# Moving the low part of half of each Q from VectorE to GpSimd in a two-layer attention kernel

## The chip, the cores and the metric

One core of one Trainium2 chip runs the program. The metric is the device time of one execution in microseconds. The kernel before took 1781.78 us, the median of three runs (1780.85, 1781.80 and 1781.78 us).

## The reference, cut to what matters

Two layers work on 1024 latent tokens and 256 context tokens of width 1024. Layer 0 is a latent attention with 16 heads. Layer 1, where the change is, is a differential attention with 8 heads:

```python
SEQ, CTX_LEN, B_HEADS, B_HEAD = 1024, 256, 8, 64
# per head two query and two key maps of 64 rows each, and values of 128 rows
q = apply_rope(q, cos, sin)          # x1*cos - x2*sin , x2*cos + x1*sin
p1 = softmax(q1 @ k1.T * HD**-0.5)   # 1024 x 1280
p2 = softmax(q2 @ k2.T * HD**-0.5)
o  = rms_norm((p1 - lam * p2) @ v)   # per head, then gate and output projection
```

The result is wanted in more exact arithmetic than one half-precision product gives. So the kernel writes each float32 operand as a sum of two 16-bit numbers, a high part H = f16(x) and a low part L = f16(x - H), and multiplies the parts that matter.

## The kernel before, in words

**How layer 1 is tiled.** Each head works through eight tiles of 128 query rows against all 1280 keys. For one tile `scores1` makes two score maps on TensorE (lines L1342 and L1343, each a product with the high parts and one with the low parts of Q), VectorE takes row maxima (L1355 for the context columns, four times L1359 for the rest, and L1361 joins them), ScalarE takes the exponentials into two tiles p of 1280 columns (L1365) with their sums, and VectorE joins the two maps into one: L1368, L1369 and L1370 make the factor, and L1371 computes p0 + factor*p1 over 1280 columns. In this text "the join" is L1371. `turn1` then transposes the joined tile on TensorE (L1378, matmuls of 128x128 in float32 from p) and splits the transposed columns into 16-bit parts: ph on ScalarE (L181) and pl on VectorE (L182). `values1` multiplies ph and pl with the values (L1386 to L1388), ScalarE scales and squares the result (L1391, L1392), GpSimd makes the norm (L159, L160, L1390) and scales the rows (L1399), and the SyncE queue writes them out (L1400). A head takes about 96 us.

**The next head's operands.** While one head's tiles run, generators make K, Q and V of the next head, and their matmuls (L185 to L187) fill TensorE between the tiles. `prod_q1` makes Q in two halves of 512 columns, b = 0 and b = 1. Each half is a bank of PSUM with 128 rows (both maps), on which `rope1` works: VectorE shuffles rows into rsw (L1242), multiplies by the cosine into rr (L1243), GpSimd multiplies rsw by the sine (L1244) and adds it (L1245). The function `fin`, which runs at a later slot of the weave, then splits rr, scaled by a column es1[h], with `split16`: ScalarE writes the high part kH (L181), VectorE writes the low part kL = rr*es - kH in one instruction (L182), and eight transfers on the SyncE queue (`dmv`, L86) copy the 64-row pieces into the tiles QS (high part, twice) and Q1 (low part, twice; the profile prints it as Q). K goes the same way at 1280 columns (`prod_k1`, KS).

**What holds the order.** The program's order on TensorE around this place is written by hand. The order on VectorE, ScalarE, GpSimd and the SyncE queue is worked out by a scheduler from the instructions and their dependencies. Each engine and the queue run in their order, so an instruction that waits holds all that stands behind it. The tiles rr, rsw, kH and kL have one buffer each: the second half's L1243 writes the same rr that the first half's split still reads, and the second half's kH and kL wait until the transfers of the first half have read them. TensorE works in eight banks of PSUM, ps_b, in turn.

**Two other users of the same engines.** The weights of the next head come on the SyncE queue (ws<-in_dw, L989), ScalarE squares them for a norm (wsq<-ws, L993) and both are split into wx and wy (L181, L182). A row of gates is collected on VectorE from further weights (L1412 loads them, L1414 is the multiplication and addition over 1024 columns).

Of the kernel before, what the change touches and what calls it, by code (L numbers as in the profile page):

```python
# [13 lines left out]
AF = mybir.ActivationFunctionType  # L14
ALU = mybir.AluOpType
# [38 lines left out]
def hybrid_kernel(  # L54
# [7 lines left out]
    pe, act, dve, pool, sp = nc.tensor, nc.scalar, nc.vector, nc.gpsimd, nc.sync  # L62
# [22 lines left out]
    def dmv(dst, src):  # L85
        sp.dma_start(dst, src)  # L86
# [92 lines left out]
    def split16(hi, lo, src, scale):  # L179

        act.activation(hi, src, AF.Copy, scale=scale)  # L181
        dve.scalar_tensor_tensor(lo, src, scale, hi, op0=ALU.mult, op1=ALU.subtract)  # L182
# [793 lines left out]
    def w1(tag):  # L976
        sh, d, b = TAG1[tag]
        return rot(place[tag], sh, d, tag, b)

    wt, un, us1, es1 = {}, {}, {}, {}  # L980
# [40 lines left out]
    def proj1(n, c0, cw):  # L1021
        w = wt[0]
        ps = bank("b")
        for k in range(KT):
            mm3(ps[:, :n], w[k][0][:, cw], w[k][1][:, cw], h1H[:, k, c0:c0 + n], h1L[:, k, c0:c0 + n],
                k == 0, k == KT - 1)
            yield ps
# [212 lines left out]
    def rope1(ps, n, cos, sin, r):  # L1240
        sw = w1("rsw")
        dve.stream_shuffle(sw[:, :n], ps, SWAP16)  # L1242
        dve.tensor_tensor(r[:, :n], ps, cos, op=ALU.mult)  # L1243
        pool.tensor_tensor(sw[:, :n], sw[:, :n], sin, op=ALU.mult)  # L1244
        pool.tensor_tensor(r[:, :n], r[:, :n], sw[:, :n], op=ALU.add)  # L1245
# [27 lines left out]
    def prod_q1(h, b, ps=None):  # L1273
        c0, n = CHUNKS[b]
        if ps is None:
            for ps in proj1(n, c0, slice(0, P)):
                yield 3 * n
        rr = w1("rr")
        c = slice(c0, c0 + n)
        rope1(ps, n, cosB[:, c], sinB[:, c], rr)  # L1280
        if b == 0:
            qt1[h] = [w1(f"Q1{m}") for m in range(2)], [w1(f"QS{m}") for m in range(2)]
        q1, qs = qt1[h]

        def fin():
            H, L = w1("kH")[:, :n], w1("kL")[:, :n]
            split16(H, L, rr, es1[h])
            for m in range(2):
                r = slice(m * HD, m * HD + HD)
                dmv(qs[m][:HD, c], H[r, :])  # L1290
                dmv(qs[m][HD:, c], H[r, :])
                dmv(q1[m][:HD, c], L[r, :])
                dmv(q1[m][HD:, c], L[r, :])

        later.append(fin)
        yield 0
# [414 lines left out]
```

## Time and profile before

| | |
|---|---|
| median of three runs | 1781.78 us |
| the profiled execution | 1781.43 us |
| its span in the profile | 1779.5 us |
| mean granted TensorE clock | 0.992 |
| busy: PE, DVE, ACT, POOL | 1664.8, 1230.8, 1119.5, 800.3 us |
| layer 1's tiles of heads 0 to 7 | about 945 to 1720 us in the span |

The profiled execution is 1.9 us longer than its span; what lies outside is the same for all sums below. PE is TensorE, PEld its weight loads, DVE VectorE, ACT ScalarE, POOL GpSimd, SPq the SyncE queue of transfers. A row of the timeline gives the start and the length in us, the engine, the line, the operation, the tiles with their sizes, and in brackets how long the engine had idled before it and for whom. A row of the waits gives the waiting instruction, whom it waited for, the sum in us, the number of waits and the longest. A row of the windows gives the stretch, its length, then busy us (and instructions) of PE, PEld, DVE, ACT and POOL, the granted clock, the DMA share and GB/s.

### The profile page before, as it was taken

The page shows a single profiled execution, that of the slowest core. Times are in us where ns is not written, and L with a number is a line of the kernel's source. Part 1 is how long each engine was busy: PE and PEld are TensorE (multiplying, and loading weights), DVE is VectorE, ACT ScalarE, POOL GpSimd, SP SyncE. Part 2 cuts the span into 40 slices and gives each one's busy share as a digit, 9 for nine tenths or more (in the row PEclk, how much of TensorE's full clock was granted, in tenths as well). Part 3 has the DMA queues.
Part 4 walks back from the last instruction along what each step waited for, and adds up shares of the span by engine and source line. Part 5 has one row for each costly group of instructions (what it writes and reads, how often), then busy time and mean ns, then how long its engine had stood idle before and what let it go on. Part 6 is the DMA issues. An engine that isn't in the chain of part 4 may idle for free. (4 is left out here: it accounts for less than half of the span.)

```text
span 1779.5 us, 36756 instructions
## 1 busy us (share of the span) xinstructions
PE 1664.8 (94%) x14564; PEld 1233.5 (69%) x14564; DVE 1230.8 (69%) x2045; ACT 1119.5 (63%) x2235; POOL 800.3 (45%) x724
## 2 busy tenths in 40 slices
PE   7999999899999998999999999999998999888998
PEld 7999966566666665577866766667675757566876
DVE  7658575665665657557747787787777777868664
ACT  2551177777777787845536676767676766758542
POOL 1532147667776676845541222222313131455454
PEclk9999999999999999999999999999999999999999
DMA  8258520111111113164432212131312122232331
GB/s 301 86 151 261 161 68 22 40 46 27 36 45 34 46 42 85 47 217 166 148 108 76 55 50 74 55 79 55 81 55 60 38 61 61 68 119 67 108 110 71
DMA packets 111225, 154.84 MB, mean 87 GB/s; under 512 B 13415, under 2 KB 84679, under 8 KB 111054
## 3 DMA queue, kind: packets, MB, share of 16 engines
q1 hardware_dynamic: 102654, 144.90, 27.1%
q10 hardware_dynamic: 8400, 7.61, 1.3%
q8 instruction: 114, 1.87, 0.5%
q14 instruction: 57, 0.47, 0.1%
HBM read 98.65 MB, written 27.07 MB: 71 GB/s over the span
## 5 line engine op out<-in xcount | busy, mean ns | idle before, releaser
L779 POOL TENSOR_TENSOR pl<-p,ph 128x1024 f16<-128x1024 f32 (+1 forms) x176 | 364.7, 2078 | 146.4 <-ACT ph L778 120.6
L1365 ACT ACTIVATE p<-ps_b,mx 128x512 f32<-128x512 f32 (+1 forms) x384 | 230.7, 618 | 84.0 <-DVE mx L1361 82.9
L777 ACT ACTIVATE p<-ps_a,esc 128x1024 f32<-128x1024 f32 (+1 forms) x176 | 189.2, 1075 | 93.2 <-PE ps_a L835 87.2
L759 DVE TENSOR_REDUCE mx<-ps_a 128x1 f32<-128x1024 f32 x128 | 155.3, 1222 | 126.9 <-PE ps_a L757 126.8
L778 ACT CAST ph<-p 128x1024 f16<-128x1024 f32 (+1 forms) x176 | 177.1, 1006 | 5.5
L1359 DVE TENSOR_REDUCE mx<-ps_b 128x1 f32<-128x512 f32 x256 | 166.0, 681 | 0.3 <-PE ps_b L1343 0.3
L848 PE MATMUL ps_d<-Vh,pl 128*128 128x65 f16 x1344 | 146.0, 194 | 3.3 <-POOL pl L779 3.3
L845 PE MATMUL ps_d<-Vh,ph 128*128 128x65 f16 x1344 | 148.1, 195 | 0.0
L847 PE MATMUL ps_d<-Vl,ph 128*128 128x64 f16 x1344 | 146.9, 193 | 0.0
L845 PEld LDWEIGHTS <-ph 128*128 128x128 f16 x1344 | 123.2, 97 | 18.0 <-issue 4.6
L1342 PE MATMUL ps_b<-KS,QS 128*128 128x512 f16 (+1 forms) x384 | 127.7, 349 | 7.5 <-DVE pl L182 4.1
L1390 POOL TENSOR_TENSOR sm<-sm,us 128x1 f32<-128x1 f32 x64 | 19.3, 302 | 252.7 <-DVE sm L1369 248.3
L847 PEld LDWEIGHTS <-ph 128*128 128x128 f16 x1344 | 123.9, 98 | 12.1
L1378 PE MATMUL ps_b<-idr,p 128*128 128x128 f32 x640 | 104.1, 278 | 29.9 <-ACT p L1365 15.7
L1343 PE MATMUL ps_b<-KS,Q 128*128 128x512 f16 (+1 forms) x384 | 130.5, 349 | 0.0
L833 PE MATMUL ps_a<-qH,KH 100*128 100x512 f16 x320 | 121.5, 380 | 9.0 <-ACT p L777 4.7
L182 DVE SCALAR_TENSOR_TENSOR pl<-ps_b,lcf,ph 128x512 f16<-128x512 f32 (+1 forms) x192 | 117.2, 654 | 13.7 <-ACT ph L181 13.6
L848 PEld LDWEIGHTS <-pl 128*128 128x128 f16 x1344 | 123.1, 97 | 4.6 <-POOL pl L779 4.6
L181 ACT ACTIVATE ph<-ps_b,lcf 128x512 f16<-128x512 f32 (+1 forms) x192 | 115.4, 649 | 17.3 <-PE ps_b L1378 17.3
L834 PE MATMUL ps_a<-qH,KL 96*128 96x512 f16 x320 | 121.3, 379 | 0.0
L835 PE MATMUL ps_a<-qL,KH 96*128 96x512 f16 x320 | 120.7, 377 | 0.0
L1378 PEld LDWEIGHTS ps_b<-idr,p 128*128 128x128 f32 x640 | 77.6, 143 | 57.1 <-ACT p L1365 24.5
(435 smaller groups left out, 5282.2 us busy)
## 6 DMA issues: line engine op xcount, KB each, us to landing
ws<-in_dw SPq DMA_DIRECT2D x28, 512.0 KB, 4.0
adw<-in_ada_w SPq DMA_DIRECT2D x24, 512.0 KB, 4.6
adaw<-in_ada_w SPq DMA_DIRECT2D x16, 512.0 KB, 7.5
g<-sg_d SPq DMA_DIRECT2D x16, 512.0 KB, 9.0
sg_d<-gg ACTq DMA_DIRECT2D x40, 128.0 KB, 3.5
o_d<-op SPq DMA_DIRECT2D x7, 640.0 KB, 3.9
xt<-in_xT SPq DMA_DIRECT2D x16, 256.0 KB, 4.6
wgs<-in_w_in SPq DMA_DIRECT2D x32, 128.0 KB, 2.3
```

Source lines behind the costliest of these rows:

```text
L759: dve.tensor_reduce(mx[:, t, 0:1], ps, axis=AX.X, op=ALU.max)
L777: act.activation(p32[:, :n], st, AF.Exp, scale=esc0)
L778: act.copy(ph[:, :n], p32[:, :n])
L779: pool.tensor_tensor(pl[:, :n], p32[:, :n], ph[:, :n], op=ALU.subtract)
L845: pe.matmul(pv[:, t, :], ph[:, ts], Vh[:, k, h, :], start=(k == kcs[0] and t == 0), stop=False, skip_group_check=True)
L847: pe.matmul(pv[:, t, :V0], ph[:, ts], Vl[:, k, h, :], start=False, stop=False, skip_group_check=True)
L848: pe.matmul(pv[:, t, :], pl[:, ts], Vh[:, k, h, :], start=False, stop=(k == NT - 1), skip_group_check=True)
L1342: pe.matmul(out, qs[m][:, ts], ks[m][:, c0:c0 + n], start=True, stop=False)
L1343: pe.matmul(out, q1[m][:, ts], ks[m][:, c0:c0 + n], start=False, stop=True)
L1359: dve.tensor_reduce(mx[:, 2 + 2 * m + i:3 + 2 * m + i], b, axis=AX.X, op=ALU.max, negate=True)
L1365: act.activation(p[m][:, c0:c0 + n], b, AF.Exp, bias=nb, accum_out=sm[:, 2 + 3 * m + i:3 + 3 * m + i])
L1378: pe.transpose(st[:, j * P:(j + 1) * P], pc[:, (k0 + j) * P:(k0 + j + 1) * P], idn)
```

## The change

In `fin` of `prod_q1`, the first half (b = 0) no longer calls `split16`. ScalarE makes the high part as before. GpSimd then scales rr in place and subtracts the high part from it. The second half stays as it was. The lines behind L1287 move down by five: the join L1371 becomes L1376, the maxima L1355, L1359 and L1361 become L1360, L1364 and L1366, the row scaling L1399 becomes L1404, its transfer L1400 becomes L1405, and the gates' L1414 becomes L1419. The code runs for eight heads, for head 0 ahead of the tiles and for heads 1 to 7 within the tiles of the head before.

```diff
         def fin():
             H, L = w1("kH")[:, :n], w1("kL")[:, :n]
-            split16(H, L, rr, es1[h])
+            if b:
+                split16(H, L, rr, es1[h])
+            else:
+                act.activation(H, rr, AF.Copy, scale=es1[h])
+                pool.tensor_scalar(rr, rr, es1[h], None, op0=ALU.mult)
+                pool.tensor_tensor(L, rr, H, op=ALU.subtract)
             for m in range(2):
```

The scheduler's order changes with it. On GpSimd, where Q of head 2 is made, these rows stand before (rr is the rotated half of Q; ss and o belong to an output tile; the last two rows are the second half's):

```order
L1245 TENSOR_TENSOR rr_14569<-rr_14569,rsw_14570 128x512
L159 TENSOR_SCALAR ss_14683<-ss_14683 128x1
L160 TENSOR_TENSOR ss_14683<-ss_14683,neghalf 128x1
L1399 TENSOR_SCALAR o_2204_14681<-o_2204_14681,ss_14683 128x128
L1244 TENSOR_TENSOR rsw_14728<-rsw_14728,sinB_12501 128x512
L1245 TENSOR_TENSOR rr_14727<-rr_14727,rsw_14728 128x512
```

and these now, at the same place:

```order
L1245 TENSOR_TENSOR rr_14571<-rr_14571,rsw_14572 128x512
L1291 TENSOR_SCALAR rr_14571<-rr_14571,es_13781 128x512
L1292 TENSOR_TENSOR kL_14601<-rr_14571,kH_14600 128x512
L159 TENSOR_SCALAR ss_14686<-ss_14686 128x1
L160 TENSOR_TENSOR ss_14686<-ss_14686,neghalf 128x1
L1404 TENSOR_SCALAR o_2204_14684<-o_2204_14684,ss_14686 128x128
L1244 TENSOR_TENSOR rsw_14731<-rsw_14731,sinB_12501 128x512
L1245 TENSOR_TENSOR rr_14730<-rr_14730,rsw_14731 128x512
```

The two new instructions stand right behind the addition that ends the rotation, and the output tile's norm and the second half's rotation stand behind them.

On VectorE at the same place, from the join of one tile to the shuffle of the second half, before:

```order
L1371 SCALAR_TENSOR_TENSOR p_2162_14437<-p_2163_14438,sm_14436,p_2162_14437 128x1280
L182 SCALAR_TENSOR_TENSOR kL_14599<-rr_14569,es_13779,kH_14598 128x512
L1355 TENSOR_REDUCE mx_14610<-ps_b_14614 128x2
L1359 TENSOR_REDUCE mx_14610<-ps_b_14620 128x1
L1359 TENSOR_REDUCE mx_14610<-ps_b_14638 128x1
L1359 TENSOR_REDUCE mx_14610<-ps_b_14624 128x1
L1359 TENSOR_REDUCE mx_14610<-ps_b_14642 128x1
L1361 TENSOR_SCALAR mx_14610<-mx_14610 128x1 x2
L182 SCALAR_TENSOR_TENSOR pl_14698<-ps_b_14699,lcf,ph_14697 128x512
L1414 SCALAR_TENSOR_TENSOR gate_12517<-ws_15465,sc,gate_12517 128x1024
L1242 STREAM_SHUFFLE rsw_14728<-ps_b_14579 128x512
```

and now:

```order
L1376 SCALAR_TENSOR_TENSOR p_2162_14439<-p_2163_14440,sm_14438,p_2162_14439 128x1280
L1360 TENSOR_REDUCE mx_14613<-ps_b_14617 128x2
L1364 TENSOR_REDUCE mx_14613<-ps_b_14623 128x1
L1364 TENSOR_REDUCE mx_14613<-ps_b_14641 128x1
L1364 TENSOR_REDUCE mx_14613<-ps_b_14627 128x1
L1364 TENSOR_REDUCE mx_14613<-ps_b_14645 128x1
L1366 TENSOR_SCALAR mx_14613<-mx_14613 128x1 x2
L1419 SCALAR_TENSOR_TENSOR gate_12517<-ws_15468,sc,gate_12517 128x1024
L182 SCALAR_TENSOR_TENSOR pl_14701<-ps_b_14702,lcf,ph_14700 128x512
L1242 STREAM_SHUFFLE rsw_14731<-ps_b_14581 128x512
```

kL has left VectorE from between the join and the maxima of the next tile, and the gates' multiplication has come ahead of pl.

On VectorE at the second half of Q of head 1, from its kL on, before:

```order
L182 SCALAR_TENSOR_TENSOR kL_13446<-rr_13417,es_12789,kH_13445 128x512
L1370 SCALAR_TENSOR_TENSOR sm_13301<-sm_13301,nlam 128x1
L1355 TENSOR_REDUCE mx_13457<-ps_b_13461 128x2
L1371 SCALAR_TENSOR_TENSOR p_1988_13302<-p_1989_13303,sm_13301,p_1988_13302 128x1280
L1359 TENSOR_REDUCE mx_13457<-ps_b_13467 128x1
```

and now:

```order
L182 SCALAR_TENSOR_TENSOR kL_13448<-rr_13419,es_12790,kH_13447 128x512
L1374 RECIPROCAL sm_13303<-sm_13303 128x2
L1360 TENSOR_REDUCE mx_13459<-ps_b_13463 128x2
L1375 SCALAR_TENSOR_TENSOR sm_13303<-sm_13303,nlam 128x1
L1364 TENSOR_REDUCE mx_13459<-ps_b_13469 128x1
L1376 SCALAR_TENSOR_TENSOR p_1988_13304<-p_1989_13305,sm_13303,p_1988_13304 128x1280
```

The join has moved behind the first L1364 (the former L1359). The second half of head 6 shows the same. In the second halves of heads 2 to 5 the join has come ahead of that L1364 instead. In head 7's first half, where kL stood between L1370 and the join, one L1364 stands there now. In head 6 the low part of K (L182, 128x1280 from kr) has moved from ahead of the join's factor to behind the first half's cosine product L1243. The order on TensorE is the same as before. On the SyncE queue the eight transfers of each half stay ahead of the output tile's L1405 and, in heads 1 to 4, of a weight load L989; one of the transfers of kH has come ahead of the first two of kL.

## The prediction

> **What bounds the kernel now.** The first view is the page's list of busy times, the second the waits, grouped by who waited for whom.
>
> ```profile
> PE 1664.8 (94%) x14564; PEld 1233.5 (69%) x14564; DVE 1230.8 (69%) x2045; ACT 1119.5 (63%) x2235; POOL 800.3 (45%) x724
> ...
> PE ps_b L1378 <- ACT p L1365: 15.7, 20, 2.0
> ...
> PE ps_b L1378 <- DVE p L1371: 8.3, 8, 4.7
> ...
> DVE kL L182 <- ACT kH L181: 21.5, 13, 3.6
> ```
>
> TensorE is busy for 94% of the span. Whatever VectorE or GpSimd gain counts only where TensorE waits for them. The transposes L1378 wait 15.7 us for exponentials and 8.3 us for joins, and VectorE stands 21.5 us at kL until ScalarE has written kH. So the change can win only where VectorE's stand at kL is passed on to L1378. The third view is the timeline at that place, here head 2, first half:
>
> ```profile
> 1073.95 1.54 DVE L1371 SCALAR_TENSOR_TENSOR p<-p,sm,p 128x1280 f32<-128x1280 f32 x1
> ...
> 1075.94 1.26 POOL L1245 TENSOR_TENSOR rr<-rr,rsw 128x512 f32<-128x512 f32 x1
> ...
> 1077.24 0.72 ACT L181 ACTIVATE kH<-rr,es 128x512 f16<-128x512 f32 x1 [3.68 <-POOL rr L1245]
> ...
> 1078.00 0.75 DVE L182 SCALAR_TENSOR_TENSOR kL<-rr,es,kH 128x512 f16<-128x512 f32 x1 [2.51 <-ACT kH L181]
> ...
> 1078.67 0.68 DVE L1355 TENSOR_REDUCE mx<-ps_b 128x2 f32<-128x512 f32 x1
> ...
> 1079.18 1.19 SPq L86 DMA_DIRECT2D Q<-kL  x2
> 1079.27 2.47 DVE L1359 TENSOR_REDUCE mx<-ps_b 128x1 f32<-128x512 f32 x4
> ...
> 1081.66 0.44 DVE L1361 TENSOR_SCALAR mx<-mx 128x1 f32<-128x1 f32 x2
> ...
> 1081.96 0.69 ACT L1365 ACTIVATE p<-ps_b,mx 128x512 f32<-128x512 f32 x1 [2.73 <-DVE mx L1361]
> ...
> 1082.68 1.27 DVE L1414 SCALAR_TENSOR_TENSOR gate<-ws,sc,gate 128x1024 f32<-128x1024 f32 x1
> 1082.79 0.44 PE L1378 MATMUL ps_b<-idr,p 128*128 128x128 f32 x2 [1.96 <-ACT p L1365]
> ```
>
> The chain reads: GpSimd's addition ends at 1077.20, kH at 1077.96, kL at 1078.75. VectorE had been free since 1075.49. The maxima behind kL end late, the exponentials start late, and TensorE waits 1.96 us. Heads 3, 4 and 5 have the same pattern.
>
> **The change, part by part.** VectorE loses eight kL of 0.75 us, which are worth only what stands behind them. ScalarE's part is the same. GpSimd gains eight scalings and eight subtractions, and the nearest rows to their prices are these:
>
> ```profile
> L1399 POOL TENSOR_SCALAR o<-o,ss x56: 612/612/1400, 978.7 to 1643.0; 128x128 f32<-128x128 f32 x56
> ```
>
> ```profile
> L999 POOL TENSOR_SCALAR uw<-uw x16: 192/192/193, 829.2 to 1546.2; 128x1 f32<-128x1 f32 x16
> ```
>
> ```profile
> L779 POOL TENSOR_TENSOR pl<-p,ph 128x512 f16<-128x512 f32 x16 | 19.6, 1223 | 0.0
> ```
>
> The subtraction has a row of its own form: 1.22 us. No row shows the scaling at 512 columns. Between 1 column (0.192 us) and 128 columns (0.612 us) a column costs 3.3 ns; 0.192 + 511 x 3.3 ns gives 1.88 us. The ends are 0.61 us, if columns past 128 cost nothing, and 2.45 us, four times the 128-column row. I take 1.88 us, since both rows of the form carry it. The Trainium skill, "GPSIMD Engine Reference", section 4.1 on engine selection, says that two-input elementwise work is about twice as slow on GpSimd as on VectorE, while one-input work goes at roughly line rate. By that the scaling would cost about as much as on VectorE, and the sum would be that of the first rival below. The two rows speak against it: 3.3 ns for each further column is more than VectorE's whole kL needs (0.75 us over 512 columns, 1.5 ns).
>
> GpSimd and VectorE hold each other up where VectorE reads two tiles from SBUF:
>
> ```profile
> 1362.78 1.55 DVE L1371 SCALAR_TENSOR_TENSOR p<-p,sm,p 128x1280 f32<-128x1280 f32 x1
> ...
> 1363.41 1.40 POOL L1399 TENSOR_SCALAR o<-o,ss 128x128 f32<-128x128 f32 x1
> ```
>
> The 0.61-us scaling of an output row stretches to 1.40 us and ends 0.48 us after the join that ran beside it. So I let such pairs run one after the other.
>
> **Heads 2, 3 and 4.** VectorE no longer stands at kL. It takes the maxima from 1075.5 on as TensorE delivers them, is through by about 1078.9, and the exponentials start at about 1079.2 instead of 1081.96. The 1.96-us wait goes. What is late next is the low part itself. kH ends at 1077.96, the scaling runs to 1079.9. The gates' L1414, now ahead of pl, gets in between the two GpSimd instructions (1.27 us, to 1081.2), and the subtraction ends at 1082.5, 3.7 us later than kL did. On the SyncE queue five transfers from there on hang behind it (0.6 us each, from 1.19 for two), then the row's L1400 and the weight load L989:
>
> ```profile
> 1083.98 0.39 SPq L989 DMA_DIRECT2D ws<-in_dw  x1
> ...
> 1087.97 1.04 ACT L993 ACTIVATE wsq<-ws 128x1024 f32<-128x1024 f32 x1
> ...
> 1092.45 0.69 ACT L1365 ACTIVATE p<-ps_b,mx 128x512 f32<-128x512 f32 x1 [1.92 <-DVE mx L1361]
> ```
>
> L989 is issued at about 1086.3 instead of 1083.98. It took 4.0 us until L993 could read it, so L993 starts at 1090.3. On ScalarE the copy and the output's L1391 and L1392 follow (with L993 some 2.2 us), and the exponentials come at 1092.5 against 1092.45. The gain is given back by the next tile: **0 us** each. A microsecond on the subtraction's end is a microsecond here, up to the wait itself: from -2.0 (scaling 0.61, and the subtraction then ahead of the gates' step) to +0.6 (2.45) per head.
>
> **Head 5** has neither a gates' step nor a weight load there.
>
> ```profile
> 1371.62 0.66 PE L1378 MATMUL ps_b<-idr,p 128*128 128x128 f32 x2 [1.97 <-ACT p L1365]
> ```
>
> ```profile
> 1370.00:1380.00 10.00, 8.38 (x68) 6.36 (x69) 7.47 (x16) 5.63 (x16) 3.09 (x3) 0.83 0.28 68
> ```
>
> Its wait of 1.97 us goes, and the window that it begins ran at a clock of 0.83, 1.7 us lost of 10. The later second half takes back an estimated 0.8 us: **-2.9 us**.
>
> **Head 1** has no such wait to win, only what comes later:
>
> ```profile
> 982.74 0.75 DVE L182 SCALAR_TENSOR_TENSOR kL<-rr,es,kH 128x512 f16<-128x512 f32 x1 [1.16 <-ACT kH L181]
> ...
> 985.15 1.28 DVE L1414 SCALAR_TENSOR_TENSOR gate<-ws,sc,gate 128x1024 f32<-128x1024 f32 x1
> ...
> 990.93 0.74 DVE L182 SCALAR_TENSOR_TENSOR kL<-rr,es,kH 128x512 f16<-128x512 f32 x1
> ...
> 992.33 1.54 DVE L1371 SCALAR_TENSOR_TENSOR p<-p,sm,p 128x1280 f32<-128x1280 f32 x1
> ...
> 994.24 0.60 PE L1378 MATMUL ps_b<-idr,p 128*128 128x128 f32 x4
> ```
>
> ```profile
> Q<-kL SPq DMA_DIRECT2D x64, 64.0 KB, 2.0
> KS<-kL SPq DMA_DIRECT2D x16, 160.0 KB, 5.2
> ```
>
> The scaling starts where kL did and ends at 984.65; the gates' L1414, 0.75 us earlier than now, comes next (to 985.9), and the subtraction ends at about 987.1. The second half's kL may write its one buffer only when the first half's transfers have read it: five at 0.6 us and 2.0 us to land, about 992.0 instead of 990.93. Then come L1355 and, newly, one L1359 of 0.6 us ahead of the join, which ends at 995.65 instead of 993.87. TensorE's transposes start there instead of at 994.24: **+1.4 us**.
>
> **Head 6** loses more order than time on GpSimd:
>
> ```profile
> 1454.91 1.54 DVE L182 SCALAR_TENSOR_TENSOR kL<-kr,kc,kH 128x1280 f16<-128x1280 f32 x1
> ...
> 1467.95 0.67 DVE L1243 TENSOR_TENSOR rr<-ps_b,cosB 128x512 f32<-128x512 f32 x1
> ...
> 1474.46 1.54 DVE L1371 SCALAR_TENSOR_TENSOR p<-p,sm,p 128x1280 f32<-128x1280 f32 x1
> ```
>
> K's low part, moved behind L1243 of the first half, ends at about 1464. Its transfers land 5.2 us later, at about 1469, and only then may the subtraction write kL; it ends at 1470.2. The second half's L1243, which overwrites rr, starts 2.3 us after its 1467.95. The join ends 1.9 us late, and 0.2 us of that is spare: **+1.7 us**.
>
> **Head 7** is the reverse:
>
> ```profile
> 1559.84 1.27 DVE L1370 SCALAR_TENSOR_TENSOR sm<-sm,nlam 128x1 f32<-128x1 f32 x1
> ...
> 1565.41 1.54 DVE L1371 SCALAR_TENSOR_TENSOR p<-p,sm,p 128x1280 f32<-128x1280 f32 x1
> ...
> 1567.01 1.11 PE L1378 MATMUL ps_b<-idr,p 128*128 128x128 f32 x4 [4.73 <-DVE p L1371]
> ```
>
> The join stood behind kL. Without it, and with one maximum of 0.6 us ahead, it starts at about 1561.9, and TensorE goes on 3.4 us earlier. As ScalarE and VectorE are then late by part of it, I count **-2.7 us**. Head 0's Q is made ahead of the tiles, and nothing waits for it: 0.
>
> **The sum**: 0 + 1.4 + 3 x 0 - 2.9 + 1.7 - 2.7 = -2.5 us. Against the profiled execution's 1781.43 us that is 1778.9; the median of the runs is 0.35 us higher, so I forecast **1779.3 us**.
>
> **The rivals.** First, **a cheap scaling**, 0.61 us. Then the subtraction ends 1.27 us earlier everywhere, and ahead of the gates' step. Heads 2 to 4 keep their 2.0 us each, head 5 2.9, head 7 3.0, and heads 1 and 6 lose only 0.4 and 1.0: -6.0 - 2.9 - 3.0 + 1.4 = -10.5 us, **1771.3 us**. For it speaks that no row shows 512 columns; against it the step from 1 to 128 columns.
>
> Second, **slower: the late weight load**. If the subtraction ends over 0.6 us later than I worked out (the scaling at 2.45 us does it), L989 lands so late that heads 2 to 4 wait anew at the next tile, 0.6 us each. A wait of about 2 us starts a stretch at low clock sometimes (head 5's window shows 0.83, while the same wait in head 2 shows 1.00 in its row below), 1.7 us each time; I count half, 0.85.
>
> ```profile
> 1076.00:1086.00 10.00, 8.04 (x61) 5.37 (x59) 7.49 (x15) 5.99 (x18) 3.85 (x5) 1.00 0.34 81
> ```
>
> That is 3 x 1.45, with 1.4 + 0.85 for head 1 and 1.7 + 0.85 for head 6, less 2.4 and 2.2 in heads 5 and 7: +4.6 us, **1786.4 us**. For it speaks that one queue carries all, against it that the gains in heads 5 and 7 don't pass over that queue.
>
> Third, **nothing is left**: heads 5 and 7 give back theirs within the next tile as heads 2 to 4 do, and heads 1 and 6 have the spare time: **1781.8 us**.
>
> **How the numbers follow.** A measurement of this kernel tells about 0.2%, 3.6 us, from no change. I give my forecast 0.45, with a range of its own from 1774.5 to 1781.5 (0.14 of it faster by over 0.2%, 0.29 within, 0.02 slower); the cheap scaling 0.22, all faster; the late load 0.25, of which 0.01 within and 0.24 slower; nothing left 0.08, within. That makes faster 0.36, same 0.38, slower 0.26. The range reaches from just below the first rival to just above the second, 1770.5 to 1787.0, which takes in both ends of the scaling.
>
> **What would show it.** Right: L1291 at about 1.9 us and L1292 at about 1.2 us; L1378's waits for exponentials in the first halves of heads 2 to 5 gone; L993 of heads 2 to 4 some 2 us later; new waits of L1378 for the join in the second halves of heads 1 and 6; head 7's 4.73 us down to about 1.3. Wrong: L1291 far from 1.9 us either way, the gates' step not between the two GpSimd instructions, or the 2-us waits standing elsewhere in the same head.

## The result and the profile after

The changed kernel takes 1776.72 us (median of eight runs, 1774.20 to 1779.27) against 1781.79 us for the kernel before (eight runs, 1780.85 to 1786.46). The ratio is 0.9968 with an interval of 0.9957 to 0.9979: 5 us less, about 0.3%. The profiled execution has a span of 1775.8 us.

The page's busy times of the changed kernel:

```profile
PE 1662.7 (94%) x14564; PEld 1232.4 (69%) x14564; DVE 1225.1 (69%) x2037; ACT 1117.2 (63%) x2235; POOL 822.2 (46%) x740
```

VectorE has lost its eight instructions and GpSimd has 22 us more. TensorE's work is the same. Next come the waits (who waited <- for whom: sum, number, longest):

```profile
DVE kL L182 <- ACT kH L181: 11.7, 8, 4.5
...
PE ps_b L1383 <- ACT rr L1313: 7.8, 4, 2.3
...
PE ps_b L1383 <- ACT p L1370: 5.2, 13, 0.9
```

L1383 is the transposes' line, which was L1378. Its waits for exponentials fell from 15.7 to 5.2 us, and the 2-us ones are gone. A new group of four waits has come instead, 7.8 us, for L1313, the copy into rr on ScalarE (line 1308 before). VectorE's stand at kL has halved. The timeline of the changed kernel at the place shown before, head 2, first half (this execution is 5.8 us later there, for reasons told below):

```profile
1083.03 0.72 ACT L1290 ACTIVATE kH<-rr,es 128x512 f16<-128x512 f32 x1 [3.68 <-POOL rr L1245]
...
1083.85 1.56 POOL L1291 TENSOR_SCALAR rr<-rr,es 128x512 f32<-128x512 f32 x1 [0.86 <-ACT kH L1290]
...
1084.20 0.44 DVE L1366 TENSOR_SCALAR mx<-mx 128x1 f32<-128x1 f32 x2
...
1084.56 1.27 DVE L1419 SCALAR_TENSOR_TENSOR gate<-ws,sc,gate 128x1024 f32<-128x1024 f32 x1
...
1085.50 1.35 POOL L1292 TENSOR_TENSOR kL<-rr,kH 128x512 f16<-128x512 f32 x1
...
1086.87 1.10 SPq L86 DMA_DIRECT2D Q<-kL  x2
...
1088.66 1.24 SPq L86 DMA_DIRECT2D Q<-kL  x2
...
1090.65 0.39 SPq L989 DMA_DIRECT2D ws<-in_dw  x1
...
1094.80 1.06 ACT L993 ACTIVATE wsq<-ws 128x1024 f32<-128x1024 f32 x1 [2.98 <-DMA ws<-in_dw]
...
1096.26 0.66 PE L1383 MATMUL ps_b<-idr,p 128*128 128x128 f32 x4 [1.66 <-ACT rr L1313]
```

The maxima are joined (L1366) while GpSimd still scales, so the exponentials and the transposes no longer wait. The low part ends at 1086.85, 3.1 us after kH. Its transfers hold the weight load L989 until 1090.65, ScalarE stands 2.98 us at L993, the copy L1313 stands behind that, and TensorE waits 1.66 us for the bank that the copy frees.

**Where the time went, stretch by stretch.** The next table splits the trace at the first scaled output (L1391, now L1396) of each head. A stretch holds the making of one head's Q. "Waits" adds TensorE's waits of over 0.15 us, "clock" is the stretches times one less their granted clock, that is, the work lost to half clock. (Some of the expectations below give these sums 0.4 to 0.7 us larger.) Each kernel has two traces: its own, and one of the experiments below.

| Q of head | before, two traces | changed, two traces | forecast | measured |
|---|---|---|---|---|
| 1 | 95.8, 95.9 | 95.8, 95.5 | +1.4 | -0.2 |
| 2 | 96.2, 96.1 | 94.6, 94.5 | 0 | -1.6 |
| 3 | 96.2, 96.1 | 95.0, 95.5 | 0 | -0.9 |
| 4 | 96.5, 96.7 | 94.8, 94.7 | 0 | -1.9 |
| 5 | 97.4, 96.4 | 94.6, 94.6 | -2.9 | -2.3 |
| 6 | 98.0, 97.8 | 99.2, 99.2 | +1.7 | +1.3 |
| 7 | 87.3, 85.7 | 83.9, 84.0 | -2.7 | -2.6 |
| none (head 7's tiles) | 116.5, 116.5 | 116.5, 116.5 | 0 | 0 |
| all | 783.9, 781.2 | 774.4, 774.5 | -2.5 | -8.1 |
| of it waits | 54.4, 53.2 | 52.0, 51.1 | | -2.2 |
| of it clock | 10.2, 10.2 | 3.4, 5.1 | | -6.0 |

Two things are to be seen. The pattern of gains and losses is the forecast one, but for heads 1 to 4. And in these traces the waits fell by only 2.2 us; three quarters of the difference is time at a lower clock. All runs together give the clock less weight: the mean granted clock is 0.9920 in the 60 runs of the kernel before that have one on record, and 0.9928 in the 13 of the changed kernel (8 here and 5 in its repeat). That is 14.2 and 12.8 us of mean spans of 1780.5 and 1774.7 us, so on average 1.4 of 5.8 us are clock (2.9 of 6.8 us in the one session that has both), and the two pairs of traces drew more.

**What lies ahead of the stretches.** The first output of head 0 comes at 976.0 and 977.5 us in the two traces of before, at 981.8 and 979.0 in those of the changed kernel, although the code of layer 0 is the same. A place where it happens, in the windows of both traces (the row's last four figures are POOL's count, the granted clock, the DMA share and GB/s), of before:

```profile
320.00:335.00 15.00, 12.12 (x154) 7.82 (x153) 10.77 (x25) 9.81 (x10) 9.28 (x6) 1.00 0.19 55
```

and of the changed kernel:

```profile
320.00:335.00 15.00, 12.12 (x116) 7.10 (x113) 8.77 (x22) 7.41 (x7) 8.35 (x5) 0.77 0.17 50
```

TensorE waits the same 1.50 and 1.38 us there in both, and in one of them runs at half clock afterwards. So part of what one execution shows against another is this draw, and so is part of the 5 us by which runs of one kernel spread. The medians, 5.1 us apart, and not the stretches alone, 8.1 us, say what the change is worth.

### The profile page after: what moved, and what is told of

It is laid out like the page before. It is cut to its first block, busy times and chain, and to the rows that moved or that the text cites. A ratio compares the mean times of both kernels' runs of the same rounds, so it can differ in the third digit from the quotient of the medians.

```text
span 1775.8 us, 36794 instructions
## 1 busy us (share of the span) xinstructions
PE 1662.7 (94%) x14564; PEld 1232.4 (69%) x14564; DVE 1225.1 (69%) x2037; ACT 1117.2 (63%) x2235; POOL 822.2 (46%) x740
## 5 line engine op out<-in xcount | busy, mean ns | idle before, releaser
L1370 ACT ACTIVATE p<-ps_b,mx 128x512 f32<-128x512 f32 (+1 forms) x384 | 230.2, 616 | 65.6 <-DVE mx L1366 64.6
L777 ACT ACTIVATE p<-ps_a,esc 128x1024 f32<-128x1024 f32 (+1 forms) x176 | 189.0, 1074 | 97.4 <-PE ps_a L835 91.3
L1364 DVE TENSOR_REDUCE mx<-ps_b 128x1 f32<-128x512 f32 x256 | 165.4, 680 | 0.4 <-PE ps_b L1348 0.3
L1383 PE MATMUL ps_b<-idr,p 128*128 128x128 f32 x640 | 102.7, 276 | 28.3 <-ACT rr L1313 7.8
L182 DVE SCALAR_TENSOR_TENSOR pl<-ps_b,lcf,ph 128x512 f16<-128x512 f32 (+1 forms) x192 | 116.8, 653 | 14.3 <-ACT ph L181 14.3
L1383 PEld LDWEIGHTS ps_b<-idr,p 128*128 128x128 f32 x640 | 77.0, 141 | 54.2 <-ACT p L1370 10.9
```

The source lines that it names most:

```text
L777: act.activation(p32[:, :n], st, AF.Exp, scale=esc0)
L1364: dve.tensor_reduce(mx[:, 2 + 2 * m + i:3 + 2 * m + i], b, axis=AX.X, op=ALU.max, negate=True)
L1370: act.activation(p[m][:, c0:c0 + n], b, AF.Exp, bias=nb, accum_out=sm[:, 2 + 3 * m + i:3 + 3 * m + i])
L1383: pe.transpose(st[:, j * P:(j + 1) * P], pc[:, (k0 + j) * P:(k0 + j + 1) * P], idn)
```

## The experiments

All were timed beside the kernel before, whose medians in these sessions were 1781.29 to 1783.14 us. In the expectations the sums, and the stretch of head 1, are 16 us larger than in the table above, since they were counted from 16 us ahead of head 0's first output. The diffs are cut to the lines that matter, against the changed kernel if nothing else is said.

**1. The changed kernel again** (an empty line added).

> The changed kernel once more, to part what belongs to it from what differs between two executions. From the first output of layer 1's head 0 (line of the scaled output on ScalarE) to the last one, the profiled execution before took 799.9 us (54.8 us of waits of TensorE, 10.9 us lost to a clock below full) plus or minus little, the one after 790.4 us (52.5 and 3.4). Theory 1, the waits moved as forecast: the waits repeat within 1 us, and the time is 1775 to 1778.5 us. Rival, the gain is luck of the clock: the waits stay near 52.5 but the clock's loss comes back to about 10 us, and the time lies at 1780 or above.

1775.64 us (1774.22 to 1778.19), ratio 0.9962 (0.9948 to 0.9976). The stretches repeat within 0.5 us, the waits are 51.1 us, and the clock takes 5.1 us. Theory 1 holds: the gain belongs to the kernel.

**2. The kernel before again** (an empty line added).

> The kernel before once more, for a second trace. Theory 1, its stretches repeat: 799 to 801 us from the first output of head 0 to the last one, with the 2-us waits in the first halves of heads 2 to 5 and the 4.7-us wait of head 7 again, whatever layer 0 does (first output at 976 to 982 us). Rival, the clock's loss of 10.9 us there was chance: another loss in those stretches, and 792 to 797 us.

One time, 1780.29 us, and a sum of stretches of 781.2 us with the same 10.2 us lost to the clock, but partly in other places. Its windows behind the 2-us waits of heads 4 and 5:

```profile
1276.00:1286.00 10.00, 9.40 (x78) 7.15 (x79) 8.66 (x16) 7.31 (x21) 3.08 (x3) 0.83 0.42 111
1373.00:1383.00 10.00, 9.71 (x96) 8.18 (x97) 8.26 (x18) 6.53 (x22) 4.46 (x6) 1.00 0.28 68
```

The wait of head 5 is the one whose window ran at 0.83 in the prediction's row; here it is at 1.00. Whether a wait of this size costs a stretch of low clock is drawn anew in each execution (five of the eight waits of 1.96 to 1.97 us in the two traces did). Both theories were half right: the waits belong to the kernel, the place of the clock's loss in heads 2 to 5 does not.

**3. No low part at all**: GpSimd's two instructions are left out, and the four transfers copy the high part.

```diff
-                pool.tensor_scalar(rr, rr, es1[h], None, op0=ALU.mult)
-                pool.tensor_tensor(L, rr, H, op=ALU.subtract)
+                L = H
```

> The changed kernel without the first half's low part: GpSimd's two instructions are left out for all heads, and the four transfers copy the high part in its place (so this half's low part is wrong). Orders on TensorE and VectorE as in the changed kernel, on ScalarE but for two rows. Theory 1, what the changed kernel gives back is the lateness of the low part: the waits at the next tile of heads 1 to 4 and 6 (2.35, 1.66, 2.04, 1.79 and 1.84 us) shrink to under 0.5 us each, 1766 to 1770 us. Rival, the weight load is late whatever the low part does (its buffer comes free late): the waits keep more than 1 us each, and the time is 1774 to 1777 us.

1771.20 us (1768.03 to 1775.04), ratio 0.9942 (0.9928 to 0.9957). The waits of heads 1 to 4 for the copy into rr, 2.35, 1.66, 2.04 and 1.79 us in the changed kernel, are 0.83 us, none, 0.61 and 0.34 us here, and the one of head 6 for the join falls from 1.84 to 0.98 us:

```profile
1466.92 0.63 PE L1383 MATMUL ps_b<-idr,p 128*128 128x128 f32 x4 [0.98 <-DVE p L1376]
```

Theory 1 holds in the main, with a time a little above its range and three of the five waits above its 0.5 us: what the change gives back, some 5 us, is the lateness of the low part, and not a weight load that is late in any case. GpSimd has less to do here too, which this experiment doesn't part from it; the twelfth does.

**4. A second scaling**, to measure the sensitivity.

```diff
                 pool.tensor_scalar(rr, rr, es1[h], None, op0=ALU.mult)
+                pool.tensor_scalar(rr, rr, 1.0, None, op0=ALU.mult)
                 pool.tensor_tensor(L, rr, H, op=ALU.subtract)
```

> A second scaling (by 1.0) on GpSimd between the scaling and the subtraction, so that the low part ends 1.56 us later, eight times; nothing else is reordered on TensorE, VectorE and ScalarE. Theory 1, the end of the subtraction sets the next tile through the SyncE queue and the weight load behind it: the new waits of heads 1 to 4 (2.35 and 1.66 us) and that of head 6 (1.84 us) grow by 1.2 to 1.6 us each, 6 to 8 us in all, 1783 to 1785 us. Rival, the low part has room and the new waits come from the order on VectorE or ScalarE alone: within 1.5 us of the changed kernel, 1775 to 1778 us.

1784.81 us (1781.55 to 1790.35), ratio 1.0013 (1.0002 to 1.0025): 8 to 9 us more than the changed kernel. Head 2 in its timeline:

```profile
1082.38 1.28 DVE L1420 SCALAR_TENSOR_TENSOR gate<-ws,sc,gate 128x1024 f32<-128x1024 f32 x1
...
1085.10 1.15 POOL L1293 TENSOR_TENSOR kL<-rr,kH 128x512 f16<-128x512 f32 x1
...
1086.28 2.38 SPq L86 DMA_DIRECT2D Q<-kL  x4
...
1089.41 0.39 SPq L989 DMA_DIRECT2D ws<-in_dw  x1
...
1095.01 1.03 PE L1384 MATMUL ps_b<-idr,p 128*128 128x128 f32 x4 [2.57 <-ACT rr L1314]
```

Counted from the gates' step, the subtraction ends 1.58 us later than in the changed kernel (3.87 against 2.29 us) and the weight load comes 0.94 us later (7.03 against 6.09); TensorE's wait is 0.91 us longer. The missing 0.64 us is one transfer: the four of the low part stand together here, while in the changed kernel one of the high part stood among them. The time is in theory 1's range, but the waits carry less than half of it: they sum to 53.8 us, 1.8 and 2.7 us more than in the changed kernel's two traces, and the clock loses 13.7 us instead of 3.4 and 5.1. Each of the waits of heads 1 to 4 (2.95, 2.57, 2.78 and 2.35 us) was followed by 3.41 us at half clock. Over its eleven runs the mean granted clock is 0.9903, 4.5 us more lost than in the changed kernel's runs, half of the difference.

**5. The low part one slot later, on VectorE**, against the kernel before. GpSimd does nothing new. The rotated half lies in K's buffer, which is free by then, and the low part in a buffer of 512 columns. In the diff, low(H) is the low part rr*es - H on VectorE with its four transfers.

```diff
+            if b or h == 0:
+                low(H)
+            else:
+                later.append(lambda: low(H))
```

> The kernel before with the low part of the first half left on VectorE, but put one slot later (behind the next tile's maxima instead of ahead of them), from a tile of its own (the rotated half lies in K's buffer, the low part in a buffer of 512 columns), for heads 1 to 7. GpSimd does nothing new. Theory 1, the gain is that VectorE no longer stands at kL, and the loss is the late low part with its one buffer: the first-half waits go as in the changed kernel, the low part is made some 2 us earlier than on GpSimd, and the waits behind it shrink: 1768 to 1774 us. Rival, the gain is VectorE's 0.75 us that GpSimd takes over: 1778 to 1782 us, as before.

1775.54 us (1773.36 to 1776.23), ratio 0.9956 (0.9942 to 0.9969), the same as the changed kernel. Head 2:

```profile
1082.93 0.75 DVE L1294 SCALAR_TENSOR_TENSOR kM<-kr,es,kH 128x512 f16<-128x512 f32 x1
...
1084.25 1.28 DVE L1427 SCALAR_TENSOR_TENSOR gate<-ws,sc,gate 128x1024 f32<-128x1024 f32 x1
1084.48 1.53 POOL L1412 TENSOR_SCALAR o<-o,ss 128x128 f32<-128x128 f32 x1
...
1086.03 0.33 SPq L1413 DMA_DIRECT2D o_d<-o  x1
...
1086.46 2.39 SPq L86 DMA_DIRECT2D Q<-kM  x4
...
1088.97 0.51 SPq L989 DMA_DIRECT2D ws<-in_dw  x1
...
1094.98 0.66 PE L1391 MATMUL ps_b<-idr,p 128*128 128x128 f32 x4 [2.00 <-ACT rr L1321]
```

So the gain is the place of the low part, behind the next tile's maxima instead of ahead of them, and not the engine. (The buffer of its own is not what gains: see the eighth.) The rival falls, but the time lies above theory 1's range too. My expectation that an earlier low part (ready at 1083.68) would shorten the next wait fell: the queue stood at the output row L1413 until 1086.03, since its scaling L1412 on GpSimd had to wait for the gates' step, and the four transfers came behind it.

**6. Heads 1 and 6 with the old split.**

```diff
-            if b:
+            if b or h in (1, 6):
```

> The changed kernel with the old split (VectorE) for heads 1 and 6. Theory 1, these two lose and the rest gains: the stretches in which Q of heads 1 and 6 is made (first output of head 0 to that of head 1, and of head 5 to head 6) are as before, 111.8 and 98.0 us, against 111.8 and 99.2 us in the changed kernel, all others as in the changed kernel (94.6, 95.0, 94.8, 94.6 and 83.9 us but for the clock): about 1 us less, 1774.5 to 1777 us. Rival, head 6 lost by chance of the clock or by what head 5 gave back: no change, or its stretch stays at 99 us.

1774.60 us (1773.06 to 1777.28), ratio 0.9951 (0.9936 to 0.9965). The stretch of head 6 is 97.9 us, as before the change; that of head 1 is 95.9, the others as in the changed kernel. Head 6's loss is its own, as theory 1 has it.

**7. The slot-later kernel without head 6.**

```diff
-            if b or h == 0:
+            if b or h in (0, 6):
```

> The low part one slot later on VectorE, GpSimd left alone, and head 6 as before. Theory 1, the gain is the place of kL behind the maxima and not the engine, and head 6 has none to give: the same as the slot-later kernel with head 6 in (1775.5 us), within 1.5 us. Rival, VectorE's 0.75 us counts as soon as head 6 doesn't lose: 1777 to 1780 us.

1774.04 us (1771.09 to 1775.82), ratio 0.9957 (0.9944 to 0.9970): within 1.5 us of the fifth, as theory 1 has it. In its trace the stretch of head 6 is 98.5 us, against 97.5 in the fifth and 97.9 before, so head 6 was not what the fifth lost by.

**8. A buffer of its own for the low part** (kM, 512 columns).

> The changed kernel with a buffer of 512 columns of its own for the first half's low part. Orders on TensorE, VectorE and ScalarE as in the changed kernel. Theory 1, the one buffer holds up heads 1 and 6 (VectorE's second kL waits 1.42 us for transfers in head 6): the stretch of head 6 falls by 1 to 1.5 us, that of head 1 by 0 to 1, 1774 to 1776 us. Rival, the cosine product that waits for the subtraction (rr) holds head 6 up just as long: no change beyond 0.5 us.

1776.46 us (1774.21 to 1781.14), ratio 0.9974 (0.9962 to 0.9985): no change, and a little above theory 1's range. Head 6's wait falls from 1.84 to 1.42 us, and its stretch from 99.2 to 99.0. The one buffer was 0.2 to 0.4 us of the loss, not 1 to 1.5.

**9. The low part's transfers issued by GpSimd**, from the buffer of its own, for the first halves of heads 1 to 7, and behind all four of the high part.

```diff
-                dmv(q1[m][:HD, c], L[r, :])
-                dmv(q1[m][HD:, c], L[r, :])
+                    (sp if b or h == 0 else pool).dma_start(q1[m][:HD, c], L[r, :])
+                    (sp if b or h == 0 else pool).dma_start(q1[m][HD:, c], L[r, :])
```

> The changed kernel with the four transfers of the first half's low part issued by GpSimd itself right behind its subtraction, from a buffer of their own, so that nothing on the SyncE queue waits for the low part. Orders on TensorE, VectorE and ScalarE as in the changed kernel but for two to four rows. Theory 1, the waits given back at the next tile (2.35, 1.66, 2.04 and 1.79 us in heads 1 to 4) come through that queue: they shrink to under 0.7 us, and the time is 1769 to 1773 us. Rival, issuing transfers costs GpSimd about 1 us each and pushes the output rows and the second half's rotation behind them: 1777 to 1785 us.

1791.69 us (1788.90 to 1795.77), ratio 1.0057 (1.0043 to 1.0070). Heads 2 and 1 (the last row):

```profile
1086.53 1.36 POOL L1292 TENSOR_TENSOR kM<-rr,kH 128x512 f16<-128x512 f32 x1
...
1088.18 0.62 POOL L1296 DMA_DIRECT2D Q<-kM  x1 [0.29 <-POOL kM L1292]
...
1089.82 0.52 POOL L1297 DMA_DIRECT2D Q<-kM  x1
...
1092.42 0.39 SPq L989 DMA_DIRECT2D ws<-in_dw  x1
...
1001.48 1.09 PE L1388 MATMUL ps_b<-idr,p 128*128 128x128 f32 x4 [6.22 <-DVE p L1381]
```

The rival's mechanism holds, at 0.52 to 0.62 us a transfer and not 1 us, and the time is above its range: from the subtraction's end (1087.89) to the end of the fourth issue (1090.34) GpSimd spends 2.45 us. The output row that L989 stands behind is scaled that much later, and the weight load, meant to be freed, comes later than ever, 4.5 us after the subtraction's end. In head 1 TensorE waits 6.22 us.

**10. The scaled half written to rsw** (sw in the code), so that the scaling need not wait until ScalarE has read rr.

```diff
-                pool.tensor_scalar(rr, rr, es1[h], None, op0=ALU.mult)
-                pool.tensor_tensor(L, rr, H, op=ALU.subtract)
+                pool.tensor_scalar(sw, rr, es1[h], None, op0=ALU.mult)
+                pool.tensor_tensor(L, sw, H, op=ALU.subtract)
```

> The changed kernel with the scaled half written to rsw (free after the addition) instead of in place, so that the scaling need not wait for ScalarE's read of rr (0.86 us, seven times). Orders on TensorE, VectorE and ScalarE as in the changed kernel. Theory 1, in heads 1 to 4 the subtraction then meets the gates' multiplication on VectorE, which reads two tiles and runs from just when the scaling ends: it waits for its end, and ends no earlier than now (within 0.2 us); the waits at the next tile stay (2.1 to 2.4, 1.5 to 1.7, 2.0 to 2.5, 1.7 to 1.8 us), and only heads 6 and 7 can gain: 1775 to 1777 us. Rival, the two engines don't hold each other up here: the subtraction ends 0.86 us earlier everywhere, and with 0.6 us of wait per us (as the second scaling showed: 0.9 us for 1.56) the four waits shrink by 0.5 us each: 1773 to 1775 us.

1778.85 us (1777.27 to 1783.85), ratio 0.9986 (0.9976 to 0.9995): 2 to 3 us slower than the changed kernel. Head 2:

```profile
1081.14 1.56 POOL L1292 TENSOR_SCALAR rsw<-rr,es 128x512 f32<-128x512 f32 x1
...
1082.59 1.28 DVE L1420 SCALAR_TENSOR_TENSOR gate<-ws,sc,gate 128x1024 f32<-128x1024 f32 x1
1082.79 2.11 POOL L1293 TENSOR_TENSOR kL<-rsw,kH 128x512 f16<-128x512 f32 x1
...
1084.92 1.10 SPq L86 DMA_DIRECT2D Q<-kL  x2
...
1086.07 1.23 SPq L86 DMA_DIRECT2D QS<-kH  x2
...
1087.35 1.24 SPq L86 DMA_DIRECT2D Q<-kL  x2
...
1089.33 0.39 SPq L989 DMA_DIRECT2D ws<-in_dw  x1
...
1095.43 0.75 PE L1384 MATMUL ps_b<-idr,p 128*128 128x128 f32 x4 [2.80 <-ACT rr L1314]
```

The subtraction starts earlier and ends no earlier, at 3.1 us after kH as in the changed kernel, since it stands until the gates' step on VectorE is over (2.11 us instead of 1.16). That is theory 1. But the wait at the next tile grew to 2.80 us, which neither theory had. The main reason is in the queue: two transfers of the high part now stand behind the first pair of the low part, so six follow the subtraction's end instead of five. The waits of heads 1 to 4 are 2.80 to 3.08 us, and behind each come 3.41 us at half clock. Over the twelve runs the mean granted clock is 0.9914 against 0.9928, which is 2.4 of the 3.3 us by which the mean span is longer.

**11. The same with the own buffer and without head 6.**

> The kernel of the run before (scaling into rsw), with the own buffer for the low part and without the change in head 6: what of the changed kernel gains, put together. Theory 1: head 6's stretch at 97.9 us instead of 99.2, the others as in the changed kernel: 1773 to 1776 us. Rival: as the changed kernel, 1775 to 1777.5 us.

1779.82 us (1777.85 to 1783.23), ratio 0.9988 (0.9980 to 0.9997). Theory 1 missed here, mainly for the tenth's reason: the stretches of heads 2 to 4 are 95.5 to 96.0 us, nearly as slow as there (95.9 to 96.2), with waits of 2.41 to 2.97 us and half clock behind each. Head 6's stretch is 98.6 us, not 97.9.

**12. The high part's transfers first.** The tenth suggested it.

```diff
             for m in range(2):
                 r = slice(m * HD, m * HD + HD)
                 dmv(qs[m][:HD, c], H[r, :])
                 dmv(qs[m][HD:, c], H[r, :])
+            for m in range(2):
+                r = slice(m * HD, m * HD + HD)
                 dmv(q1[m][:HD, c], L[r, :])
                 dmv(q1[m][HD:, c], L[r, :])
```

> The changed kernel with all four transfers of the high part ahead of the four of the low part on the SyncE queue (in the changed kernel one of them, in the run with rsw two, stood behind the first two of the low part). Orders on TensorE, VectorE, ScalarE and GpSimd as in the changed kernel. Theory 1, each transfer between the subtraction's end and the weight load costs 0.6 us of the load: L989 comes 0.6 us after the end of the subtraction sooner than the changed kernel's 3.8 us, the waits at the next tile of heads 1 to 4 fall from 2.35, 1.66, 2.04 and 1.79 us by 0.4 to 0.7 us each: 1773.5 to 1775.5 us. Rival, the load's landing, not its issue, sets ScalarE: the waits stay within 0.2 us, 1775.5 to 1777 us.

**1770.43 us** (1768.42 to 1772.17), ratio 0.9935 (0.9921 to 0.9948): faster than both kernels, below theory 1's range, and as fast as the third experiment, which has no low part at all (0.9928 to 0.9957). Head 2:

```profile
1081.69 1.35 POOL L1292 TENSOR_TENSOR kL<-rr,kH 128x512 f16<-128x512 f32 x1
...
1083.07 2.38 SPq L86 DMA_DIRECT2D Q<-kL  x4
...
1086.20 0.39 SPq L989 DMA_DIRECT2D ws<-in_dw  x1
...
1091.57 0.66 PE L1385 MATMUL ps_b<-idr,p 128*128 128x128 f32 x4 [0.79 <-ACT rr L1315]
```

From the subtraction's end to the weight load it is 3.16 us here with four transfers between them, 3.80 us in the changed kernel with five, and 4.43 us in the tenth with six: 0.63 us each. The waits of heads 1 to 4 are 1.58, 0.79, 1.22 and 1.00 us, each 0.8 to 0.9 us less, a little more than theory 1 has it. The stretches sum to 770.4 us against 774.4 and 774.5, the waits to 48.9 against 52.0 and 51.1. The median fell by 5 to 6 us, by more than the waits. Most of it is clock: over the five runs the mean granted clock is 0.9950 against 0.9928, 4.0 of the 6.0 us between the mean spans.

## Why the prediction was right, and where its terms were off

The forecast was 1779.3 us, a small gain made of gains and losses; the median is 2.6 us below it, on the same side. The bound and the chain behind the new waits were right. That the sum came so near is in part luck: head 1's loss didn't come, heads 2 to 4 gained, head 7's number came about by other parts, and the clock moved in places that the sum didn't have.

**The bound was right.** TensorE's waits at the transposes set the stretches, the stand of VectorE at kL was passed on to them, and the 2-us waits of heads 2 to 5 went as forecast.

**By the prediction's own signs** it was half right. The waits for exponentials in heads 2 to 5 went, and head 6 has its new wait for the join. But the scaling took 1.56 us and not 1.9, the gates' step did not stand between the two GpSimd instructions, and 1.66 to 2.35 us of waits came in heads 1 to 4 at the next tile; L993 of head 2 started 1.0 us later, not some 2.

**Heads 2 to 4: the mechanism was right, the size off.** The late low part does hold up the weight load on the SyncE queue and L993 on ScalarE, and the next tile pays, as the experiments without a low part and with the high part first show. But the term was 0 us each, and measured were -1.6, -0.9 and -1.9. The mis-sized step is the end of the subtraction, put 4.5 us after kH (1082.5 against 1077.96) and measured at 3.1 us. The scaling takes 1.56 us, not the 1.88 of the line through two rows, and the subtraction 1.16 us where nothing holds it. The two rows were not of one form: L999 scales by constants, L1399 by a column. The form with a column takes 0.267 us for one column of data (L1092), which with L1399's 0.612 gives 1.66 us. Above all the gates' step does not get in between the two: it ran while the scaling still went on. So L989 came 0.9 us later than before instead of 2.3 (1090.65 against 1083.98, this execution being 5.8 us later there). The 4.0 us from L989 to L993 were read from a row in which L993 stood behind kH and not for its load; here, where it stands for the load, they are 4.15.

Of the three gains only a part is waits. TensorE's waits in these stretches were 6.8, 6.9 and 6.0 us before (5.7, 5.7 and 6.1 in the second trace) and are 5.6, 5.9 and 5.7 us (5.4, 5.4 and 5.6): 0.4 to 0.8 us less each. The rest is half clock, 1.7 us of work each time, which was lost in four of these six stretches before and in one of six after. The waits' part fits the lateness: the subtraction came 1.4 us sooner than worked out, and the second scaling showed 0.6 us of wait per us (0.91 for 1.58), not the full microsecond that I counted.

Where the page "GPSIMD Engine Reference" of the Trainium skill, section 4.1, has one-input work at roughly line rate, the measured 1.56 us for 512 columns is twice VectorE's 0.75 us for its whole low part, and the measurement decides.

**Head 5: right**, -2.3 us against -2.9. Its waits fell from 5.4 and 5.8 to 2.8 us, and the 1.7 us of clock that I counted were lost in one of the two traces before.

**Head 7: the number right (-2.6 against -2.7), by luck in its parts.** The 4.73-us wait became three, of 0.94, 1.41 and, in the second half, 1.42 us:

```profile
1563.01 0.66 PE L1383 MATMUL ps_b<-idr,p 128*128 128x128 f32 x4 [0.94 <-DVE p L1376]
...
1565.73 0.66 PE L1383 MATMUL ps_b<-idr,p 128*128 128x128 f32 x4 [1.41 <-ACT o L1396]
...
1577.08 0.63 PE L1383 MATMUL ps_b<-idr,p 128*128 128x128 f32 x4 [1.42 <-DVE p L1376]
```

The first of them is smaller than the 1.3 us that I expected, but the other two take most of the gain back. The stretch's waits fell only from 14.2 and 14.8 to 13.1 and 13.3 us, while its clock loss fell from 6.8 and 5.1 to 3.4 us: the half clock that followed the 4.73-us wait in both traces (3.4 and 1.7 us) is gone. I had counted waits there and no clock.

**Head 6: right in its size (+1.3 against +1.7), partly in its chain.** The changed kernel's timeline there:

```profile
1467.17 0.61 POOL L1404 TENSOR_SCALAR o<-o,ss 128x128 f32<-128x128 f32 x1
...
1468.94 0.69 DVE L1243 TENSOR_TENSOR rr<-ps_b,cosB 128x512 f32<-128x512 f32 x1 [1.32 <-POOL kL L1292]
...
1472.82 0.75 DVE L182 SCALAR_TENSOR_TENSOR kL<-rr,es,kH 128x512 f16<-128x512 f32 x1 [1.42 <-DMA Q<-kL]
...
1476.58 0.63 PE L1383 MATMUL ps_b<-idr,p 128*128 128x128 f32 x4 [1.84 <-DVE p L1376]
```

The second half waits for the subtraction, then for the one buffer, and TensorE for the late join, as forecast. The transfers of K, which I had ahead of all this, did not hold up the subtraction: K's low part ended at 1460.67, not 1464. GpSimd's order did. In head 6 the subtraction does not stand right behind the scaling: an output row's norm and scaling (L159, L160 and L1404, 1466.23 to 1467.78) stand between them, and it ends 4.4 us after kH instead of 2.9 to 3.1.

**Head 1: wrong.** The term was +1.4, measured -0.2. The subtraction ended at 991.44, 1.5 us sooner than I had it (987.1, this execution being 5.8 us later), and the second half's join was not late. Its own first-half waits of 0.75 and 0.23 us go, and its new wait is the weight load's, like in heads 2 to 4, and not the join's:

```profile
1001.17 0.66 PE L1383 MATMUL ps_b<-idr,p 128*128 128x128 f32 x4 [2.35 <-ACT rr L1313]
```

**The clock.** I counted 1.7 us of it, in head 5 only. The traces show 10.2 us lost in the stretches before, twice, and 3.4 and 5.1 us after, but over all runs the two kernels lose 14.2 and 12.8 us of their whole spans, as said above. So the clock's part in the change is 1 to 3 us, near what I counted, though not where I counted it; single traces don't show it well. The Trainium skill ("TensorE: Matmul & The Clock Gate", Part 1, "What's actually happening") describes an activity window that runs free and does not start with the kernel. The traces agree, as far as they go: the same 1.97-us wait of head 5 was followed by a window at 0.83 in one execution and at 1.00 in another.

**The same terms at the lateness that I had assumed.** The second scaling ends the low part about 4.7 us after kH, near my 4.5. There the stretches of heads 1 to 4 are 97.1, 95.6, 95.8 and 95.5 us, by the means of before +1.2, -0.5, -0.3 and -1.1, nearer to the forecast's +1.4 and three times 0. But each of the four holds 1.7 us of clock, which the forecast didn't have there, so this supports the step and doesn't prove it. Heads 5, 6 and 7 (96.2, 100.8 and 85.0 us) then keep 0.7, lose 2.9 and keep 1.5 us, and the kernel is slower than before (1.0002 to 1.0025), not 2.5 us faster: at the lateness that I had assumed, the sum would have been too hopeful.

**The rivals.** The cheap scaling was not it (1.56 us is nearer to 1.88 than to 0.61). The late weight load was the right mechanism for a slower kernel, and the second scaling shows it, but in the changed kernel the subtraction ended sooner than I worked out and not later, so it did not decide. Nothing left falls too: heads 5 and 7 kept theirs.

## What to carry to other kernels

An instruction that stands at a semaphore costs what is queued behind it, so ask first whether it can stand elsewhere in the order: here the same engine one slot later gained as much as the other engine did. When work moves to a slower engine, follow its output through the in-order queue that carries it. Here each transfer between the late result and the weight load behind it cost 0.63 us of the load, and putting the ready transfers first was worth about as much again as the change itself (ratio 0.9935 against 0.9968). And a longer wait can cost clock besides: the mean granted clock was 0.9890 over the runs of the ninth experiment, with its wait of 6.22 us, and 0.9950 over those of the twelfth, whose waits at the next tile are the shortest of the kernels with a low part on GpSimd.

## What the runs showed of the hardware that I had not expected

In these traces the length of a wait goes with what TensorE's clock does behind it. Counted are TensorE's waits of 0.7 us and more in the stretches of heads 1 to 6 of all fourteen traces, and whether half clock began within 7 us of the wait's start. Of the 184 below 1.9 us none was followed by half clock, of the 36 between 1.9 and 2.4 us 13 were, and of the 16 from 2.40 us on all were, for 3.41 us each, or 6.83 behind the two longest (3.86 and 6.22 us). In head 7, where waits stand close together, half clock also came behind waits of 1.4 us.

GpSimd's scaling holds VectorE's two-input work up only in its first part, as far as the spans of GpSimd, which are rough, show it. In head 1 of the changed kernel the gates' step started 0.27 us into the scaling and took 1.49 us, 0.22 us longer than alone; in head 2 (shown above) it started 0.71 us in and took its usual 1.27 us, while the scaling went on:

```profile
988.63 1.56 POOL L1291 TENSOR_SCALAR rr<-rr,es 128x512 f32<-128x512 f32 x1 [0.86 <-ACT kH L1290]
...
988.90 1.49 DVE L1419 SCALAR_TENSOR_TENSOR gate<-ws,sc,gate 128x1024 f32<-128x1024 f32 x1
```

By these rows it lets go after about 0.5 us of its 1.56 (an estimate, 0.27 + 0.22). A two-input product of GpSimd held on to its end here, where VectorE's small L1375 (0.2 us alone) ends with L1244:

```profile
1183.11 1.26 POOL L1244 TENSOR_TENSOR rsw<-rsw,sinB 128x512 f32<-128x512 f32 x1
...
1183.68 0.71 DVE L1375 SCALAR_TENSOR_TENSOR sm<-sm,nlam 128x1 f32<-128x1 f32 x1
```

And a transfer that GpSimd issues takes 0.52 us of GpSimd's own time, 0.62 for the first of four (0.76 in head 1).
